# Residual stores on ScalarE's queue, and five smaller moves in a two-layer hybrid decoder step on one core

## The chip, the cores and the metric

The kernel runs on one core of one Trainium2 chip. The metric is device time in microseconds (us) of one execution, the median of several runs. Engines are named as in the profile: PE (matmul), PEld (PE's weight loads), DVE (vector), ACT (scalar, activations), POOL (GpSimd) and SP (here only an issuer of DMAs). A chip run of this kernel that differs by less than 0.3% (7.6 us) from another can't be told from it.

## The reference

One inference step of a two-layer decoder over 1032 tokens (1024 of a prompt, 8 samples of one token each), model width 1024, in float32:

```python
for l in range(DEPTH):                       # DEPTH = 2
    hn = _rmsnorm(x, norm_mix_g[l])
    if l < N_A:                              # layer 0: RG-LRU
        u = hn @ w_in_a[l]
        gate, xr, qm = u[..., :768], u[..., 768:1536], u[..., 1536:]
        xr, rc = _causal_dwconv(xr, rnn_conv0[l], ...)   # width 4
        y, hl = _rglru(xr, rnn_h0[l], ...)   # gates, a scan over tokens
        main = y * gelu(gate)
    else:                                    # layer 1: window-128 attention
        ...
    mem = _mem_attn(qm, mem_k[l], mem_v[l])  # 4 heads over 256 memory rows
    x = x + concat(main, mem) @ w_out[l]     # 1024 x 1024, the residual
    hn = _rmsnorm(x, norm_ffn_g[l])
    u = _causal_dwconv(hn @ w_ffn_up[l])     # 1024 x 6144, conv of width 3
    x = x + (gelu(u[..., :3072]) * u[..., 3072:]) @ w_ffn_down[l]
```

Beside the output of the trunk, the recurrent states (`yl`, the last conv inputs, and `rl`, the last scan values), the conv states and the keys and values are outputs of their own. The samples attend to memories of their own (`cache_mem_k`, `cache_mem_v`).

## The kernel before

**Arithmetic.** A float32 product runs as three matmuls in a reduced float32 type: an operand is split into a high part (a copy on ACT, `acopy`, L105) and a low part (the rest, a subtract on DVE, `vtt`, L113, or on POOL, `gtt`, L116). `mm3` then issues high by high (L298), high by low (L299) and low by high (L300). So each weight and each activation has to be loaded, copied by ACT and subtracted by DVE or POOL before PE can use it. A weight (`get`, `w_load` L251, `w_split`) is loaded up to two weights ahead by SP and split one ahead: its low part is always POOL's.

**Order.** One program, written as Python generators. `tick()` moves every open generator to its next `yield`, and one generator of a background list too. That order is the scheduler's input; for DVE, PE, POOL and SP (and ACT in the middle of layer 1) a scheduler then lines the instructions up, and on ACT in layer 0 and both FFNs they stay in the order of the program (`act_in_order(True)`). An engine runs its line in order, and so does SP with the DMAs that it issues: one that waits holds back all behind it. Big tiles (128 x 1032, "row") come from one pool of 44 buffers.

**Stages** (us of the profiled execution). Layer 0's RNN, 190 to 335: for six tiles of 128 channels the dense products of both branches, conv, gates and scan. Beside it the background list runs `sample_mem` (the samples' memory attention: scores, a transpose, a softmax on 32 rows, a second transpose on PE at L729, a masked copy on DVE, then products with the values, L749) and `ffn_prep`. Then `out_proj(0)`, 335 to 516; layer 0's FFN to 1250, its up-projection ending at about 1000; layer 1's mixer to 1624, `out_proj(1)` to 1779, and layer 1's FFN with its up-projection's end at about 2250.

**`out_proj`.** For each half of the tokens (`hb`), each of 8 output tiles `m` and each of two quarters `q` (258 columns): `get` the weight `m`, load the residual tile `x[m]` (in layer 0 by L772 from `x_t`, 516 KB; only in the first half), 24 matmuls, `vtt` of the sum into `x[m]` on DVE, then `on_tile`: a store of these 128 x 258 to `rD` in DRAM (L1323, 64 of them in both layers), a Square on ACT, and its sum on DVE. After a half, `norm(hf)` begins: it sums over partitions with a matmul by ones (L1335), takes the inverse root, scales, adds and splits the operands of the FFN (a chain of DVE, ACT and POOL), while the second half of `out_proj` runs on PE. `rD` is read back only at the FFN's end (`refill`).

**The last steps of the up-projection.** While its last tile's seven products run (`i` from 0 to 6), `fetch` loads the gated rows `gD[0]` to `gD[5]`, and `gated(j)` splits them for the down-projection: high on ACT, low on DVE (128 x 1032); the first down weight `dn.0.0` is loaded and split at step 4.

**Layer 1's mixer rows.** `load_m(b)` loads the mixer's output of token block `b` (0, 1, 2) from `mD` (L1820) and splits it. `mgetB` asks for a block when `out_proj(1)` first comes to its columns.

Of the kernel before, what the change touches and what calls it, by code (L numbers as in the profile page):

```python
# [18 lines left out]
NT = SEQ + NB  # L19
# [10 lines left out]
TIL = ((0, 1, 2), (3, 4, 5), (6, 7))  # L30
# [6 lines left out]
DCH = 6  # L37
# [12 lines left out]
def tile_trunk(ctx: ExitStack, tc: tile.TileContext, I: dict, O: list):  # L50
    nc = tc.nc
    mul, add, sub, amax = ALU.mult, ALU.add, ALU.subtract, ALU.max
# [31 lines left out]
    def ps():  # L84
        return pp.tile([P, 512], F32, tag="ps", name=nm("ps"))
# [26 lines left out]
    def vtt(out, a, b, op):  # L112
        return V.tensor_tensor(out=out, in0=a, in1=b, op=op)  # L113
# [12 lines left out]
    def f(ap):  # L126
        return ap.bitcast(F32)
# [22 lines left out]
    def spawn(g):  # L150
        t = Task(g)
        tasks.append(t)
        return t
# [116 lines left out]
    def get(key, ahead=1, load=1):  # L270
        i = widx[key]
        if Prep.fences and i >= Prep.fences[0]:
            Prep.fences.pop(0)
        end = (Prep.fences[0] if Prep.fences else len(W)) - 1
        top = min(end, i + ahead)
        while Prep.split <= top:
            while Prep.loaded <= min(end, Prep.split):
                w_load(Prep.loaded)
                Prep.loaded += 1
            w_split(Prep.split)  # L280
            Prep.split += 1
        while Prep.loaded <= min(end, top + load):
            w_load(Prep.loaded)
            Prep.loaded += 1
        return W[i]["t"]

    def load_w(n):
        while Prep.loaded < n:
            w_load(Prep.loaded)
            Prep.loaded += 1  # L290
# [399 lines left out]
    def sample_mem(l, dst):  # L690
        ck, cv = I["cache_mem_k"][l], I["cache_mem_v"][l]
        sc = sm()
        for hf in range(2):
            qb = row()
            SY.dma_start(qb[:, :1024], dbc(qmD[l][4 * hf : 4 * hf + 4, :], P, 1024))
            for pr in range(2):
                b0 = 4 * hf + 2 * pr
                kt = row()
                k4 = kt[:, :1024].rearrange("p (b k f) -> p b k f", b=2, k=2)
                for j in range(2):  # L700
                    SY.dma_start(k4[:, j], ck[b0 + j].rearrange("(k p) h d -> p k (h d)", p=P))
                yield
                for j in range(2):
                    q1 = qb[:, (2 * pr + j) * 256 : (2 * pr + j + 1) * 256]
                    gtt(k4[:, j], k4[:, j], q1[:, None, :].to_broadcast([P, 2, 256]), mul)
                yield
                for j in range(2):
                    V.tensor_reduce(
                        out=sc[:, :64].rearrange("p (k r) -> p k r", k=2)[:, :, (b0 + j) * 4 : (b0 + j) * 4 + 4],
                        in_=k4[:, j].rearrange("p k (h d) -> p k h d", h=4),  # L710
                        axis=AX.X,
                        op=add,
                    )
                yield
        yield
        yield
        t = ps()
        for k in range(2):
            T.transpose(t[:32, k * P : (k + 1) * P], sc[:, k * 32 : (k + 1) * 32], ident)
        yield  # L720
        n_, den, rd, pt = ty(), ty(), ty(), sm()
        V.tensor_reduce(out=n_[:32, :1], in_=t[:32, :256], axis=AX.X, op=amax, negate=True)
        act(pt[:32, :256], t[:32, :256], AF.Exp, bias=n_[:32, :1], accum_out=den[:32, :1])
        V.reciprocal(out=rd[:32, :1], in_=den[:32, :1])
        ts(V, pt[:32, :256], pt[:32, :256], rd[:32, :1], None, mul, None)
        yield
        t = ps()
        for k in range(2):
            T.transpose(t[:, k * 32 : (k + 1) * 32], pt[:32, k * P : (k + 1) * P], ident[:32, :32])  # L729
        bm32 = sm()  # L730
        SY.dma_start(bm32[:, :256], I["c_bm32"])
        pm = row()
        m4 = pm[:, :512].rearrange("p (k b r) -> p k b r", k=2, b=8)
        bm = bm32[:, :256].rearrange("p (b r) -> p b r", b=8)
        for k in range(2):
            vtt(m4[:, k], t[:, None, k * 32 : (k + 1) * 32].to_broadcast([P, 8, 32]), bm, mul)
        yield
        oc = sm()
        for pr in range(4):
            vt = row()  # L740
            v4 = vt[:, :1024].rearrange("p (b k f) -> p b k f", b=2, k=2)
            for j in range(2):
                SY.dma_start(v4[:, j], cv[2 * pr + j].rearrange("(k p) h d -> p k (h d)", p=P))
            yield
            yield
            o = ps()
            for j in range(2):
                for k in range(2):
                    T.matmul(  # L749
                        o[:32, :256], m4[:, k, 2 * pr + j], v4[:, j, k],  # L750
                        start=j == 0 and k == 0, stop=j == 1 and k == 1,
                    )
            for h in range(4):
                oh = o[:32, h * 64 : (h + 1) * 64]
                if pr == 0 and h == 0:
                    ts(V, oc[:32, :64], oh, hm32[:32, 0:1], None, mul, None)
                else:
                    stt(oc[:32, :64], oh, hm32[:32, h : h + 1], oc[:32, :64], mul, add)
            yield
        t = ps()  # L760
        T.transpose(t[:64, :32], oc[:32, :64], ident[:32, :32])
        t3 = t[:64, :32].rearrange("p (b h) -> p h b", h=4)
        for h in range(4):
            V.tensor_copy(out=dst(h), in_=t3[:, h])
        yield
# [9 lines left out]
    def out_proj(l, mget, ks, x, on_tile, on_half):  # L775
        for hb in range(2):
            for m in range(KD):
                key = f"out{l}.{hb}.{m}"
                wh, wl = get(key, 1, 1)
                if x[m] is None:  # L780
                    x[m] = residual(l, m)
                for q in (2 * hb, 2 * hb + 1):
                    c0 = QB[q]
                    p = ps()
                    mm3(p[:, :QW], [(wh[:, k * P : k * P + P], wl[:, k * P : k * P + P]) + mget(k, c0, QW) for k in ks])
                    vtt(x[m][:, c0 : c0 + QW], x[m][:, c0 : c0 + QW], p[:, :QW], add)
                    on_tile(q, m)
                    tick()
                drop(key)
            on_half(hb)  # L790
# [67 lines left out]
    def ffn(l, x, ops, need, weights, on_block, store=None):  # L858
# [84 lines left out]
        def gated(j):  # L943
            a = ga.pop(j)
            gh[j], gl[j] = row(F32R), row(F32R)
            acopy(gh[j][:, :NT], a[:, :NT])
            vtt(gl[j][:, :NT], a[:, :NT], f(gh[j][:, :NT]), sub)

        def refill(m):
            x[m] = row()  # L950
# [5 lines left out]
        for q, (j, name, hfs) in enumerate(SEQUENCE):  # L956
            if q == 6:
                load_pair(1)
            want = 7 if q < 10 else min(len(todo), q - 7 + AHEAD)
            while at < want:  # L960
                combine(*todo[at])
                at += 1
            t = product(j, name, hfs)
            if t is not None:
                last.append(t)
            tick()
            if j == KF - 1:
                i = STEADY.index(name)
                if i < DCH:
                    fetch(i)  # L970
                if i > 1:
                    gated(i - 2)
                if i == 4:
                    get(f"dn{l}.0.0", 0, 1)

        def down(c, m, b):
# [307 lines left out]
        tick()  # L1284
    bgfinish(smp)

    SY.dma_start(O[1], yl)
    SY.dma_start(O[2], rl)
    Mh, Ml = {}, {}
    ks_a = (6, 7, 0, 1, 2, 3, 4, 5)  # L1290

# [18 lines left out]
    def enter_ffn(l, x, mh, ml):  # L1310
# [8 lines left out]
        def cols(q):  # L1319
            return slice(QB[q], QB[q] + QW)  # L1320

        def on_tile(q, m):
            SY.dma_start(rD[l, m, :, cols(q)], x[m][:, cols(q)])  # L1323
            if m == 0:
                sums[q] = sm()
                act(sums[q][:, :QW], x[m][:, cols(q)], AF.Square)
            else:
                t = sm()
                act(t[:, :QW], x[m][:, cols(q)], AF.Square)
                vtt(sums[q][:, :QW], sums[q][:, :QW], t[:, :QW], add)  # L1330
# [95 lines left out]
    x = [None] * KD  # L1426
    ot, oh, need, ops, uw = enter_ffn(0, x, Mh, Ml)
    out_proj(0, mgetA, ks_a, x, ot, oh)
    Mh, Ml = {}, {}


# [401 lines left out]
    def start_m(b):  # L1833
        if b not in mload:
            while not {(i, e) for i in TIL[b] for e in range(2)} <= swa_done:
                tick()
            if b == 2:
                bgfinish(sst)
            mload[b] = spawn(load_m(b))
# [7 lines left out]

    x = [None] * KD
    start_m(0)
    get("out1.0.0", 1, 1)  # L1850
    for _ in range(6):
        tick()
# [139 lines left out]
```

## Time and profile before

| | before |
|---|---|
| median of 3 runs (lowest, highest) | 2533.32 us (2533.03, 2538.68) |
| the profiled execution: its time, its span | 2532.97 us, 2531.2 us |
| PE busy | 2336.5 us, 92% of the span |
| DVE, POOL, ACT busy | 61%, 56%, 44% |
| chain that ended last: PE, DVE, ACT | 34%, 7%, 2% |
| DMA moved | 273.64 MB, mean 108 GB/s |

The span is that of the trace; the 1.8 us between it and the time lie outside of the recorded work. PE's busy share is a mean over stages that differ: the views that follow cut the span into these stages.

### The profile page before, as it was taken

Reading aid. Unit: us, or ns where it says so; the run is one execution under the profiler, and the core shown is the slowest. Engines: PE = TensorE matmul, PEld = TensorE weight load, DVE = VectorE, ACT = ScalarE, POOL = GpSimd, SP = SyncE. Lnnn points to the kernel's source line nnn. Section 1 sums busy time; section 2 is a strip of 40 time slices with the busy share of each in tenths; the row PEclk is TensorE's granted clock in tenths of the full one; section 3 lists DMA queues with packets and bytes.
Section 4 is the critical chain, followed back from the end, with each engine's and each line's share of the span. In section 5 each row is a group of like instructions: output and inputs, shape, how many; then the busy total and the mean of one; then the engine's idle time right before and its main releaser. Section 6 shows DMA issues by size and latency. Waiting matters only on the chain. (4 is left out here: it accounts for less than half of the span.)

```text
span 2531.2 us, 42857 instructions
## 1 busy us (share of the span) xinstructions
PE 2336.5 (92%) x16590; PEld 2251.5 (89%) x16590; DVE 1549.6 (61%) x2826; ACT 1103.5 (44%) x2277; POOL 1428.0 (56%) x1123
## 2 busy tenths in 40 slices
PE   7997877799999999999989988787999999999999
PEld 5896866799999999999977787677999999999999
DVE  6658955666666666332478789875666566663321
ACT  5567753344433444211365577643443444442110
POOL 2149843588888885322144346435888888853220
PEclk9998989899999999999999999899999999999999
DMA  4221124212222225421575543551222222253311
GB/s 163 87 69 56 58 83 143 63 67 84 84 85 76 76 76 199 150 95 52 178 252 162 185 152 129 163 157 63 77 86 82 76 76 76 76 224 123 101 55 63
DMA packets 142491, 273.64 MB, mean 108 GB/s; under 512 B 28544, under 2 KB 85456, under 8 KB 142288
## 3 DMA queue, kind: packets, MB, share of 16 engines
q1 hardware_dynamic: 142288, 270.91, 31.9%
q8 instruction: 130, 2.13, 0.3%
q14 instruction: 73, 0.60, 0.1%
HBM read 211.99 MB, written 58.87 MB: 107 GB/s over the span
## 5 line engine op out<-in xcount | busy, mean ns | idle before, releaser
L116 POOL TENSOR_TENSOR row<-row,row 128x512 fp32r<-128x512 f32 (+9 forms) x754 | 1153.8, 1552 | 793.9 <-ACT row L105 476.4
L298 PE MATMUL ps<-row,row 128*128 128x258 f32 (+4 forms) x5032 | 1510.4, 303 | 55.5 <-ACT row L105 45.7
L299 PE MATMUL ps<-row,row 128*128 128x258 f32 (+4 forms) x5032 | 1509.1, 302 | 22.5 <-DVE row L113 18.7
L300 PE MATMUL ps<-row,row 128*128 128x258 f32 (+4 forms) x5032 | 1472.7, 301 | 23.5 <-POOL row L116 23.5
L298 PEld LDWEIGHTS ps<-row,row 128*128 128x128 f32 x5032 | 962.3, 191 | 73.9 <-ACT row L105 51.0
L299 PEld LDWEIGHTS ps<-row,row 128*128 128x128 f32 x5032 | 964.0, 192 | 40.2 <-DVE row L113 24.3
L300 PEld LDWEIGHTS ps<-row,row 128*128 128x128 f32 x5032 | 948.4, 192 | 34.1 <-POOL row L116 27.1
L105 ACT ACTIVATE row<-row 128x512 fp32r<-128x512 f32 (+8 forms) x768 | 505.4, 696 | 911.7 <-POOL row L116 305.4
L113 DVE TENSOR_TENSOR row<-row,ps 128x258 f32<-128x258 f32 (+2 forms) x736 | 322.3, 444 | 706.0 <-PE ps L300 666.5
L119 DVE SCALAR_TENSOR_TENSOR row<-row,fw,row 128x1023 f32<-128x1023 f32 x192 | 266.9, 1409 | 67.3 <-ACT row L105 67.3
L113 DVE TENSOR_TENSOR row<-row,row 128x258 fp32r<-128x258 f32 (+8 forms) x262 | 232.9, 912 | 31.3 <-ACT row L105 18.0
L105 ACT ACTIVATE row<-ps 128x258 f32<-128x258 f32 (+6 forms) x430 | 157.5, 406 | 69.6 <-PE ps L300 25.8
L116 POOL TENSOR_TENSOR row<-row,ty 128x768 f32<-128x768 f32 (+2 forms) x56 | 77.2, 1378 | 155.1 <-DVE ty L413 51.3
L105 ACT ACTIVATE row<-row,fw 128x1032 f32<-128x1032 f32 x96 | 114.9, 1245 | 68.8 <-DVE row L113 68.7
L105 ACT ACTIVATE sm<-row 128x258 f32<-128x258 f32 (+3 forms) x130 | 54.5, 452 | 153.5 <-DVE row L113 127.2
L113 DVE TENSOR_TENSOR row<-row,sb 128x8 f32<-128x8 f32 x96 | 102.3, 1066 | 0.0
L113 DVE TENSOR_TENSOR sm<-sm,sm 128x258 f32<-128x258 f32 (+5 forms) x125 | 81.9, 660 | 28.2 <-ACT sm L105 25.7
L105 ACT ACTIVATE row<-ps,ty,ty 128x256 f32<-128x256 f32 (+1 forms) x160 | 87.4, 564 | 10.1 <-DVE ty L113 7.6
L105 ACT ACTIVATE sm<-ps 128x384 f32<-128x384 f32 (+5 forms) x156 | 65.0, 444 | 39.2 <-PE ps L431 21.6
L113 DVE TENSOR_TENSOR row<-ps,row 128x384 fp32r<-128x384 f32 (+2 forms) x125 | 63.5, 519 | 25.1 <-ACT row L105 10.2
L119 DVE SCALAR_TENSOR_TENSOR row<-sm,pack,row 128x384 f32<-128x384 f32 (+1 forms) x54 | 62.6, 1162 | 14.6 <-POOL row L124 13.3
L116 POOL TENSOR_TENSOR sm<-sm,row 128x192 f32<-128x192 f32 (+3 forms) x72 | 49.5, 702 | 36.1 <-ACT sm L105 18.6
(163 smaller groups left out, 1497.3 us busy)
## 6 DMA issues: line engine op xcount, KB each, us to landing
row<-in_w_ffn_up SPq DMA_DIRECT2D x96, 512.0 KB, 3.3
gD<-row SPq DMA_DIRECT2D x48, 516.0 KB, 2.6
row<-gD SPq DMA_DIRECT2D x48, 516.0 KB, 5.6
row<-in_w_ffn_down SPq DMA_DIRECT2D x64, 384.0 KB, 3.1
row<-hD SPq DMA_DIRECT2D x48, 512.0 KB, 6.6
row<-in_w_out SPq DMA_DIRECT2D x32, 512.0 KB, 4.2
rD<-row SPq DMA_DIRECT2D x64, 129.0 KB, 1.9
row<-rD SPq DMA_DIRECT2D x16, 516.0 KB, 8.7
```

What stands on the lines that cost most here:

```text
L105: return nc.scalar.activation(out, in_, func, **kw)
L113: return V.tensor_tensor(out=out, in0=a, in1=b, op=op)
L116: return G.tensor_tensor(out=out, in0=a, in1=b, op=op)
L119: return V.scalar_tensor_tensor(out=out, in0=a, scalar=s, in1=b, op0=op0, op1=op1)
L298: T.matmul(out, ah, bh, start=first and j == 0, stop=False, skip_group_check=more)
L299: T.matmul(out, ah, bl, start=False, stop=False, skip_group_check=more)
L300: T.matmul(out, al, bh, start=False, stop=last and j == n - 1, skip_group_check=more)
```

## The change

Six edits, numbered here. (1) `sample_mem` (both layers) yields twice more between the softmax and the second transpose. (2) `gated(j)` does the low part of `j` = 0, 2, 4 on POOL, not on DVE. (3) `dn.0.0` and the weight after it are loaded from step 1 of the last tile, and `dn.0.0` is split at step 5. (4) The 64 stores to `rD` are issued by ACT, not by SP. (5) The stores of `yl` and `rl` stand behind `out_proj(0)` in the program. (6) In layer 1 a watcher generator starts `load_m(1)` and `load_m(2)` as soon as their rows are there.

```diff
@@ sample_mem
         ts(V, pt[:32, :256], pt[:32, :256], rd[:32, :1], None, mul, None)
+        yield
+        yield
         yield
         t = ps()
@@ ffn: gated, and the last tile of the up-projection
-            vtt(gl[j][:, :NT], a[:, :NT], f(gh[j][:, :NT]), sub)
+            (gtt if j < DCH and j % 2 == 0 else vtt)(gl[j][:, :NT], a[:, :NT], f(gh[j][:, :NT]), sub)
...
-                if i == 4:
+                if i == 1:
+                    load_w(widx[f"dn{l}.0.0"] + 2)
+                if i == 5:
                     get(f"dn{l}.0.0", 0, 1)
@@ ahead of out_proj(0)
-    SY.dma_start(O[1], yl)
-    SY.dma_start(O[2], rl)
     Mh, Ml = {}, {}
@@ enter_ffn: on_tile
-            SY.dma_start(rD[l, m, :, cols(q)], x[m][:, cols(q)])
+            nc.scalar.dma_start(rD[l, m, :, cols(q)], x[m][:, cols(q)])
@@ behind out_proj(0)
+    SY.dma_start(O[1], yl)
+    SY.dma_start(O[2], rl)
@@ layer 1, ahead of out_proj(1)
     start_m(0)
+
+    def ask_m():
+        for b in (1, 2):
+            while b not in mload:
+                if {(i, e) for i in TIL[b] for e in range(2)} <= swa_done and (b == 1 or sst.done):
+                    start_m(b)
+                else:
+                    yield
+
+    spawn(ask_m())
```

What the scheduler makes of it on the engines' lines (numbers in names are buffers, and differ between the kernels; lines of the kernel after the change are two to four higher).

SP's line at the start of `out_proj(0)`, before: `in_w_out` are its weights, `in_x_t` the residual tiles, `out<-yl` the state's store.

```order
L251 DMA row_3496<-in_w_out 128x1024
L1287 DMA out<-yl 128x54
L772 DMA row_3498<-in_x_t 128x1032
L1323 DMA rD<-row_3498 128x258 x2
L251 DMA row_3599<-in_w_out 128x1024
L772 DMA row_3601<-in_x_t 128x1032
L1323 DMA rD<-row_3601 128x258 x2
L251 DMA row_3667<-in_w_out 128x1024
L772 DMA row_3669<-in_x_t 128x1032
```

The same place of SP's line after the change.

```order
L251 DMA row_3491<-in_w_out 128x1024
L774 DMA row_3493<-in_x_t 128x1032
L804 DMA row_3528<-in_ffn_state 128x768
L1431 DMA out<-yl 128x54
L807 DMA out<-row_3528 1024x1x48
L251 DMA row_3597<-in_w_out 128x1024
L774 DMA row_3599<-in_x_t 128x1032
L251 DMA row_3665<-in_w_out 128x1024
L774 DMA row_3667<-in_x_t 128x1032
```

No store stands between the loads any more, and the first residual load stands ahead of the store of `yl`, which is still early. The stores now stand on ACT's line, each right ahead of the Square of its tile.

PE's line in the RNN stage, before: `ps_2693` takes the second transpose of `sample_mem`, `ps_2701` is a dense product, `ps_2674` and `ps_2680` are gates.

```order
L299 MATMUL ps_2674<-sm_2534,row_2374 128x384
L300 MATMUL ps_2674<-sm_2533,row_2374 128x384
L299 MATMUL ps_2680<-sm_2534,row_2374 128x384
L300 MATMUL ps_2680<-sm_2533,row_2374 128x384
L729 MATMUL ps_2693<-pack,sm_2623 128x32 x2
L298 MATMUL ps_2701<-row_126,row_2361 128x264
L299 MATMUL ps_2701<-row_134,row_2361 128x264
```

And where that transpose (now L731, `ps_2820`) stands after the change.

```order
L300 MATMUL ps_2761<-row_133,row_2546 128x384
L298 MATMUL ps_2801<-sm_2686,row_2558 128x384
L298 MATMUL ps_2807<-sm_2686,row_2558 128x384
L731 MATMUL ps_2820<-pack,sm_2623 128x32 x2
L298 MATMUL ps_2828<-row_126,row_2545 128x384
L299 MATMUL ps_2828<-row_134,row_2545 128x384
```

It moved back by 56 rows, behind the dense product of 264 columns, the gates of that block (`ps_2725`, `ps_2730`) and a dense product of 384 columns.

POOL's line at the end of layer 0's up-projection after the change: `row_10323` is the last up weight, `row_10457` and `row_10519` are low parts of down weights, the 128x1032 subtracts are `gated(0)`, `gated(2)` and `gated(4)`.

```order
L116 TENSOR_TENSOR row_10323<-row_10142,row_10323 128x512
L116 TENSOR_TENSOR row_10355<-row_10280,row_10354 128x1032
L116 TENSOR_TENSOR row_10421<-row_10352,row_10420 128x1032
L869 COPY ul<-row_10273 128x10
L116 TENSOR_TENSOR row_10457<-row_10318,row_10456 128x768
L869 COPY ul<-row_10311 128x10
L116 TENSOR_TENSOR row_10496<-row_10418,row_10495 128x1032
L116 TENSOR_TENSOR row_10519<-row_10320,row_10518 128x768
```

Before, none of the three 128x1032 subtracts stood there; all six were on DVE's line, which now has those of `gated(1)`, `gated(3)` and `gated(5)`.

## Rows read from the trace of the kernel before

**Rows 1.** Windows: from:to, length; busy of PE, PEld, DVE, ACT, POOL; PEclk; DMA.

```profile
600.00:650.00 50.00, 50.00 (x418) 50.00 (x417) 31.19 (x41) 22.07 (x36) 44.03 (x36) 1.00 0.18 64
190.00:335.00 145.00, 113.58 (x647) 105.17 (x647) 131.44 (x159) 113.58 (x161) 119.23 (x112) 0.91 0.18 55
335.00:412.00 77.00, 54.55 (x385) 51.59 (x386) 30.93 (x57) 23.35 (x49) 30.43 (x17) 0.85 0.42 130
412.00:516.00 104.00, 78.13 (x515) 72.95 (x515) 76.72 (x144) 40.49 (x98) 54.49 (x47) 0.83 0.24 76
976.00:1004.00 28.00, 23.65 (x159) 22.99 (x158) 20.65 (x28) 14.18 (x18) 11.92 (x7) 0.94 0.70 251
1624.00:1678.00 54.00, 49.71 (x384) 48.14 (x385) 38.24 (x74) 22.48 (x43) 22.66 (x13) 0.95 0.87 257
```

**Rows 2.** PE's waits, whole span: waited for, us in total, times, longest.

```profile
PE ps L300 <- POOL row L116: 23.5, 15, 5.0
PE ps L729 <- DVE sm L123: 12.6, 1, 12.6
```

**Rows 3.** SP's DMA issues, timeline from 335: start, length with its wait.

```profile
344.77 0.34 SPq L1287 DMA_DIRECT2D out<-yl  x1
345.21 0.38 SPq L772 DMA_DIRECT2D row<-in_x_t  x1
350.11 10.50 SPq L1323 DMA_DIRECT2D rD<-row  x2
360.70 0.38 SPq L251 DMA_DIRECT2D row<-in_w_out  x1
361.18 0.41 SPq L772 DMA_DIRECT2D row<-in_x_t  x1
366.67 0.80 SPq L1323 DMA_DIRECT2D rD<-row  x2
```

**Rows 4.** DVE and ACT, timeline from 349 to 368; in brackets the idle before.

```profile
349.65 0.42 DVE L113 TENSOR_TENSOR row<-row,ps 128x258 f32<-128x258 f32 x1 [3.64 <-DMA row<-in_x_t]
359.85 0.41 DVE L113 TENSOR_TENSOR row<-row,ps 128x258 f32<-128x258 f32 x1
366.21 0.76 DVE L113 TENSOR_TENSOR row<-row,ps 128x258 f32<-128x258 f32 x2 [5.96 <-DMA row<-in_x_t]
...
366.67 0.75 ACT L105 ACTIVATE sm<-row 128x258 f32<-128x258 f32 x2 [5.01 <-DVE row L113]
367.33 1.04 ACT L105 ACTIVATE row<-row 128x1024 fp32r<-128x1024 f32 x1
```

**Rows 5.** POOL and PE in the same half, timeline.

```profile
361.74 2.35 POOL L116 TENSOR_TENSOR row<-row,row 128x1024 fp32r<-128x1024 f32 x1 [2.11 <-ACT row L105]
...
364.14 0.39 PE L300 MATMUL ps<-row,row 128*128 128x258 f32 x1 [1.69 <-POOL row L116]
...
400.22 0.39 PE L300 MATMUL ps<-row,row 128*128 128x258 f32 x1 [1.12 <-POOL row L116]
411.56 1.66 PE L1335 MATMUL ps<-sm,ones 128*128 128x258 f32 x3 [5.79 <-DVE sm L113]
```

**Rows 6.** RNN stage, timelines of POOL and PE.

```profile
244.04 5.77 POOL L116 TENSOR_TENSOR sm<-row,sm 128x264 fp32r<-128x264 f32 x1 [0.88 <-ACT sm L105]
...
250.01 0.42 PE L729 MATMUL ps<-pack,sm 32*128 32x32 f32 x2 [12.59 <-DVE sm L123]
```

**Rows 7.** End of layer 0's up-projection, timelines of PE and DVE.

```profile
982.90 0.36 PE L298 MATMUL ps<-row,row 128*128 128x258 f32 x1 [2.00 <-DVE row L113]
...
978.66 3.77 DVE L113 TENSOR_TENSOR row<-row,row 128x1032 fp32r<-128x1032 f32 x2 [0.73 <-ACT row L105]
982.35 0.41 DVE L113 TENSOR_TENSOR row<-row,ps 128x258 f32<-128x258 f32 x1
982.68 1.22 DVE L113 TENSOR_TENSOR row<-row,row 128x1032 fp32r<-128x1032 f32 x1
```

**Rows 8.** Layer 1's `out_proj`, PE's timeline at the end of its first half.

```profile
1677.74 1.23 PE L1335 MATMUL ps<-sm,ones 128*128 128x258 f32 x2 [3.40 <-DVE sm L113]
```

## The prediction

> **What bounds the kernel now.** I read the windows by stage first, then PE's list of waits, then the timelines of the engines that release PE. In the middle of the FFN PE is busy for 50.00 of 50 us at the full granted clock, 1.00 (2.4 GHz) [rows 1]. The FFN's two long stretches can't be made faster by any of the six edits, since these change neither the number of matmuls nor their size. That leaves the places where PE stands idle: 31.4 us of the 145 us of the RNN stage, 22.5 of the 77 us of the first half of `out_proj(0)`, 25.9 of the 104 us of its second half, 4.3 of the 28 us at the up-projection's end in layer 0 (I count layer 1's like it), 4.3 of the 54 us of the first half of `out_proj(1)` [rows 1]. What one edit is worth is read from the wait that ends last in its own stage.
>
> The first half of `out_proj(0)` is the largest of them. A quarter tile is 24 matmuls; at full clock 418 take 50 us [rows 1], so 0.120 us each and 48 x 0.120 = 5.74 us for an output tile `m`. But the first matmul with the low weight (L300) of `m` = 2 starts at 364.14 and that of `m` = 7 at 400.22 [rows 5]: 36.08 / 5 = 7.22 us a tile. Both wait for POOL, as do those between them. That is not because POOL is busy: it has just waited for ACT, and takes 2.35 us [rows 5]. ACT's copy of the weight stands behind two Squares, the Squares wait for DVE's adds, and the adds wait 5.96 us for the residual tile's load [rows 4]. SP explains the load: it issues it at 361.18, because the pair of stores ahead of it held the queue from 350.11 for 10.50 us, until DVE's second add at 359.85 [rows 3, 4]. So it is a ring: store of `m` waits for the add of `m`, the load of `m`+1 waits behind the store, and the add of `m`+1 waits for the load, some 5 us after its issue.
>
> **Edits 4 and 5, in the first half of `out_proj(0)`.** SP's line now has the loads without stores between them. Three pieces:
> - The first residual load was issued at 345.21, right behind the store of `yl` at 344.77, and DVE waited for it until 349.65, idle for 3.64 us [rows 3, 4]. The load now stands ahead of that store. PE's tile must also be done; I take 3.0 of the 3.64. The splits of `Mh` and `Ml`, behind the Square on ACT, move up with it.
> - Five tiles at 7.22 us go to what sets them next. The chain from DVE's add is add 0.41, store's issue 0.40 (0.80 for two on SP [rows 3]; ACT's own price no row shows), Square 0.38 (0.75 for two), copy 1.04, POOL 2.35 [rows 4, 5]: 4.6 us, under PE's 5.74. So PE sets the pace: 5 x (7.22 - 5.74) = 7.4 us.
> - Before the sum over partitions PE waits 5.79 us (L1335 at 411.56 [rows 5]) because the last tile's load is late as well. Without that: add, issue, Square and DVE's sum, about 0.4 each, 1.6 us, and some 0.8 for semaphores: 2.4. Gain 3.4.
>
> Together 13.8 us. PE's own pace with the small waits inside a tile is probably nearer 6.2 than 5.74, which takes 2.3 back and more at the first tiles, where buffers are still scarce: I take **-11**. Bounds: -14 (all of it) and -3 (the first piece alone, if the loads then wait for buffers).
>
> The Trainium skill speaks against this term: in "DMA: Bandwidth & Descriptors", section "Issuing engines are not separate DMA queues", it says that DMAs started by several engines run on the same 16 DMA engines, and that spreading them saves only the sequencer's time to initiate them. By that alone the second and third piece would be nothing. The trace of before agrees about the transfers and shows what the sentence leaves out: the issuer holds up what stands behind a waiting DMA, 10.50 us at one pair.
>
> **The second halves, and ACT's new work.** The stores now stand on ACT's line, each ahead of the Square of the same tile. Both wait for the same add, so no new wait arises, only the issue: 16 in a half, 16 x 0.40 = 6.4 us. In the second half of `out_proj(0)` ACT is busy for 40.49 of 104 us [rows 1]; DVE, with 76.72, carries the chain of the norm. I take **0** here; bounds -2 and +6.4.
>
> **Edit 1, the second transpose.** PE stands for 12.59 us in front of it, until 250.01 [rows 2, 6]. It moves 56 rows back, behind a 264-column product and its gates. But the whole stall won't go: POOL makes the low part for that very block's gates from 244.04 to 249.81 [rows 6], so PE, in order, would next wait there, and DVE and POOL are busy for 131.44 and 119.23 of the stage's 145 us [rows 1]; DVE, nearly full, has its own work to finish before the stage ends. What PE gains is late next at DVE's scans. I take **-3**; bounds 0 and -12.6.
>
> **Edit 6, `out_proj(1)`.** Block 2's rows come earlier, inside the first half rather than at its end. PE is idle there for 4.3 of 54 us, with the DMA engines busy for 0.87 of the time, and waits 3.40 us at the end [rows 1, 8]. The stores on ACT free SP here too, but SP is not what PE waits for. I take **-2**; bounds -5 and +6.4 (16 issues on ACT).
>
> **Edits 2 and 3, the up-projection's ends.** PE waits 2.00 us at 982.90 for DVE, whose add at 982.35 came behind two low parts of 3.77 us in all [rows 7]; one alone takes 1.22 [rows 7], so one was stretched. Three of six low parts go to POOL, where the nearest row has 2.35 us (128 x 1024 [rows 5]). POOL is busy for 11.92 of these 28 us [rows 1], so it has the room. DVE loses 3 x 1.22 = 3.7 us, and the wait may shrink by 1 to 2. Against it: the low part of `dn.0.0` now stands behind two of them on POOL, 4.7 us later, and the low part of `gated(4)` comes 2.35 - 1.22 = 1.1 us later, just when PE comes to the first down-product. I take +0.5 a layer, **+1**; bounds -4 and +7.
>
> Here a rule weighs on the sum. The row shows two DVE subtracts of one form taking 3.77 us where 2 x 1.22 = 2.4 is expected [rows 7]. The Trainium skill, "SBUF — State Buffer", section "Who interferes with whom", calls DVE's second port pair shared with GpSimd, and an exclusive lock for whole instructions; the stretched row agrees. By that, each POOL low part holds DVE back.
>
> **Layer 1's mixer** is reordered by the scheduler around the two yields and the watcher. No row prices it: 0, and as bound a third of the largest single wait in PE's list, 12.6 / 3 = 4 us either way [rows 2].
>
> **Sum.** -11 + 0 - 3 - 2 + 1 + 0 = -15. The profiled execution took 2532.97 us, with a span of 2531.2, and lies 0.35 us under the median: 2533 - 15 = **2518 us**.
>
> **The rivals.**
> - *The transpose's stall goes whole.* For it: the gate behind it might find its operands, since POOL's 5.77 us there is itself a stretched row [rows 6], and a shifted DVE order might not stretch it. Against: DVE's busy share of 91%. 12.6 instead of 3: 2508 us.
> - *DVE is held by POOL at the two ends.* Three POOL subtracts block DVE for 3 x 2.35 = 7.1 us and take 3.7 of DVE's work away: +3.4 a layer, +6.8 instead of +1: 2524 us. For it: the stretched row [rows 7]. Against: POOL's first two run while PE still has products to do.
> - *The stores' move frees nothing but the first piece.* The loads then wait for buffers or for the adds, or the ring passes through ACT instead: -3 for -11, 2526 us, within 0.3% of before. For it: the chain of 4.6 us is close to 5.74, so an ACT issue of 1.5 us would close the ring again. Against: the adds wait for the load and for nothing else [rows 4]. The rule on issuing engines cited above would have it so.
> - *Slower: the issues lie on ACT's path in all halves.* ACT runs in order here and every weight split and norm split stands behind them. 64 x 0.40 = 25.6 us on the path, over the -15: 2543.6 us. It decides from 22.6 / 64 = 0.35 us a store on the path. For it: in the second halves ACT's copies release PE. Against: ACT is idle for 63.5 of 104 us there [rows 1], and in the first halves PE's 5.74 us cover the chain.
>
> **How the numbers follow.** My forecast has 0.54, the whole stall 0.10, the lock 0.10, no gain from the stores 0.17, slower 0.09. With 0.3% (7.6 us) as what a measurement can tell, faster means under 2525.7: 0.54 + 0.10 + 0.10 = 0.74; same 0.17; slower 0.09. The range, 2504 to 2532, holds the first four cases with the bounds of the reordering about them, 4 us below 2508 and 6 above 2526, and leaves out the slower case and the tails.
>
> **What would show it.** In the first half of `out_proj(0)`: L300 periods of 5.7 to 6.3 us without waits for POOL, DVE's adds released by PE and not by the load, L1335 about 11 us earlier, measured from the end of the RNN stage. ACT's stores at about 0.4 us each. At L731 a wait under 4 us, and the next wait at the gates of the same block. At the up-projection's ends PE idle within 1 us of before. The prediction is wrong if ACT's issue takes over 1 us, if the RNN stage ends later though the transpose no longer waits, or if layer 1's mixer differs by more than 4 us.

## The result, and the profile after

The changed kernel takes 2518.52 us (median of 4 runs, 2515.71 to 2519.54); the kernel before, run beside it, 2533.18 us. The ratio is 0.9935 with a 95% interval of 0.9918 to 0.9952, 12.2 to 20.8 us less; the medians are 14.7 us apart. Forecast were 2518 us and 2504 to 2532. The profiled execution has a span of 2517.7 us, 13.5 under that of before.

First the windows of the changed kernel, moved with its stages ([rows 1] are those of before; columns as there).

```profile
190.00:333.00 143.00, 114.37 (x638) 104.89 (x636) 128.30 (x157) 114.83 (x164) 116.79 (x106) 0.91 0.18 58
333.00:396.00 63.00, 54.18 (x387) 52.15 (x386) 34.78 (x60) 22.06 (x46) 27.90 (x16) 0.85 0.56 195
396.00:501.00 105.00, 77.12 (x511) 71.88 (x511) 76.49 (x145) 41.00 (x98) 54.25 (x46) 0.84 0.15 49
959.50:987.50 28.00, 25.33 (x180) 24.25 (x179) 22.57 (x26) 13.52 (x16) 17.32 (x10) 1.00 0.72 252
```

PE does the same 54 us of work in the first half of `out_proj(0)`, in 63 instead of 77 us. The second half is no shorter. At the up-projection's end PE is busy for 25.33 of 28 us, against 23.65.

How the difference is spread can be worked out from the starts of the same matmuls in both traces. The table has stage lengths; the last columns are of experiments that follow (differences from the profiled execution of before, us).

| stage, ended by | before | changed | stores alone | loads ahead, SP | changed, stores on SP | changed, layer 1 without yields |
|---|---|---|---|---|---|---|
| to the first matmul of `out_proj(0)` | 335.28 | -2.27 | -0.41 | -0.82 | -2.24 | -1.86 |
| first half, to the first L1335 | 76.28 | -13.78 | -10.33 | -10.00 | -4.27 | -15.28 |
| second half, to the first up-product | 75.19 | +1.58 | +0.85 | -0.04 | +0.38 | +1.48 |
| up-projection, to 75 us ahead of its end | 427.52 | +0.37 | +0.77 | +1.10 | -0.30 | +0.09 |
| its end, to the 61st down-product | 121.32 | -2.55 | -1.25 | -1.00 | -2.39 | -2.55 |
| rest of the FFN and layer 1's mixer | 579.29 | +6.90 | +2.94 | +2.79 | +10.52 | +2.78 |
| `out_proj(1)`, both halves | 133.44 | -1.55 | -3.19 | -0.33 | -3.66 | -1.73 |
| layer 1's up-projection, without its end | 428.43 | +0.01 | -0.32 | -0.23 | -0.40 | +0.16 |
| its end | 107.63 | -2.07 | -0.05 | -1.36 | -2.68 | -2.59 |

The first half of `out_proj(0)` in the changed kernel: SP's loads, ACT with its stores, DVE's adds, PE (start, length, in brackets the idle before and what ended it).

```profile
323.91 0.38 SPq L774 DMA_DIRECT2D row<-in_x_t  x1
...
341.57 0.34 SPq L1431 DMA_DIRECT2D out<-yl  x1
343.43 0.46 SPq L774 DMA_DIRECT2D row<-in_x_t  x1
350.29 0.33 SPq L774 DMA_DIRECT2D row<-in_x_t  x1
351.20 0.37 SPq L774 DMA_DIRECT2D row<-in_x_t  x1
...
366.35 0.33 ACTq L1325 DMA_DIRECT2D rD<-row  x1
...
343.52 0.42 DVE L113 TENSOR_TENSOR row<-row,ps 128x258 f32<-128x258 f32 x1 [1.18 <-PE ps L300]
363.25 0.42 DVE L113 TENSOR_TENSOR row<-row,ps 128x258 f32<-128x258 f32 x1 [1.70 <-PE ps L300]
368.99 0.42 DVE L113 TENSOR_TENSOR row<-row,ps 128x258 f32<-128x258 f32 x1 [1.39 <-PE ps L300]
374.75 0.43 DVE L113 TENSOR_TENSOR row<-row,ps 128x258 f32<-128x258 f32 x1 [1.41 <-PE ps L300]
...
358.80 0.58 PE L300 MATMUL ps<-row,row 128*128 128x258 f32 x1 [1.69 <-POOL row L116]
389.20 0.28 PE L300 MATMUL ps<-row,row 128*128 128x258 f32 x1
395.51 0.70 PE L1337 MATMUL ps<-sm,ones 128*128 128x258 f32 x2 [0.85 <-DVE sm L113]
```

No add waits for a load any more (where a wait is shown, it is for PE); before, an add waited 5.96 us for its load [rows 4]. The adds of the first quarters of `m` = 2, 3 and 4 (363.25, 368.99 and 374.75) stand 5.74 and 5.76 us apart: PE's own pace. In `m` = 2 PE still waits 1.69 us for POOL. The first residual load is issued at 323.91, ahead of the store of `yl`, and the others well ahead of their use; a store costs ACT 0.33 us, and the wait ahead of the partition sum (now L1337) is 0.85 instead of 5.79 us [rows 5].

PE's waits in the RNN stage, at the up-projection's end and in layer 1's mixer of the changed kernel.

```profile
241.88 0.81 PE L298 MATMUL ps<-sm,row 128*128 128x264 f32 x2 [4.49 <-ACT sm L105]
264.95 0.81 PE L298 MATMUL ps<-sm,row 128*128 128x264 f32 x2 [3.75 <-ACT sm L105]
332.85 0.23 PE L763 MATMUL ps<-pack,sm 32*64 32x32 f32 x1 [6.71 <-DVE row L113]
...
967.76 0.36 PE L298 MATMUL ps<-row,row 128*128 128x258 f32 x1 [0.93 <-DVE row L113]
983.64 0.44 PE L298 MATMUL ps<-row,row 128*128 128x384 f32 x1 [1.42 <-ACT row L105]
...
1398.75 1.02 PE L751 MATMUL ps<-row,row 128*32 128x256 f32 x4 [3.62 <-DMA row<-in_cache_mem_v]
```

The 12.59 us in front of the transpose [rows 6] are gone; 4.49 us of it came back at once at the gates behind it, and 3.75 at another block's. The 6.71 us at the stage's end are not new: before, PE waited there as long, one matmul later. At the up-projection's end PE waited three times before: 2.00 us [rows 7], and twice at the first down-products. The rows of before:

```profile
335.28 0.58 PE L298 MATMUL ps<-row,row 128*128 128x258 f32 x1 [6.60 <-ACT row L105]
...
997.34 0.45 PE L299 MATMUL ps<-row,row 128*128 128x384 f32 x1 [0.78 <-DVE row L113]
1002.48 0.44 PE L300 MATMUL ps<-row,row 128*128 128x384 f32 x1 [1.58 <-POOL row L116]
```

The 2.00 us became 0.93; the 0.78 and 1.58 are gone, and a wait of 1.42 us for ACT and a short one (0.19, shown further below) are new. The last row of the changed kernel is new too: PE waits for the samples' values, which it didn't before.

### The profile page after: what moved, and what is told of

Its sections match the earlier page's. It is cut to its first block, busy times and chain, and to the rows that moved or that the text cites. A ratio compares the mean times of both kernels' runs of the same rounds, so it can differ in the third digit from the quotient of the medians.

```text
span 2517.7 us, 42880 instructions
## 1 busy us (share of the span) xinstructions
PE 2337.0 (93%) x16590; PEld 2253.7 (90%) x16590; DVE 1558.1 (62%) x2820; ACT 1104.2 (44%) x2277; POOL 1440.6 (57%) x1129
## 5 line engine op out<-in xcount | busy, mean ns | idle before, releaser
L116 POOL TENSOR_TENSOR row<-row,row 128x512 fp32r<-128x512 f32 (+9 forms) x760 | 1166.9, 1558 | 777.5 <-ACT row L105 464.7
L300 PE MATMUL ps<-row,row 128*128 128x258 f32 (+4 forms) x5032 | 1470.6, 301 | 16.8 <-POOL row L116 16.8
L300 PEld LDWEIGHTS ps<-row,row 128*128 128x128 f32 x5032 | 946.6, 192 | 27.6 <-POOL row L116 20.1
```

What stands on the lines that cost most here:

```text
L116: return G.tensor_tensor(out=out, in0=a, in1=b, op=op)
L300: T.matmul(out, al, bh, start=False, stop=last and j == n - 1, skip_group_check=more)
```

## The experiments

Each kernel was run beside the kernel before; ratios are to that one, with their 95% interval in brackets. The intervals come from several runs of each kernel, so they can separate differences below the 0.3% of a single run. Stage lengths are from one profiled execution of each kernel.

**Edit 4 alone.**

```diff
-            SY.dma_start(rD[l, m, :, cols(q)], x[m][:, cols(q)])
+            nc.scalar.dma_start(rD[l, m, :, cols(q)], x[m][:, cols(q)])
```

> The kernel before with edit 4 alone: the 64 stores to rD are issued by ACT. Theory (the stores' wait held the residual and weight loads on SP's queue): the period of an output tile in the first half of out_proj(0) falls from 7.22 to about 5.75 us and the wait of 5.79 us ahead of the partition sum goes, so about 11 us less in that half; the first residual load still stands behind the store of yl, so the first add still waits for its load. In all 2533 - 11 = about 2522 us; the up-projection's ends and layer 1's mixer as before. Rival (the stores' move frees nothing, since all DMAs share the same engines, and the gain came from the other edits): 2530 to 2533 us.

2522.55 us, 0.9951 (0.9935 to 0.9966). The first half is 10.3 us shorter, as the theory says; the rival falls. The changed kernel has 3.5 us beyond it in this half; here the first residual load still stands behind the store of `yl` (later runs bear on that).

**Edit 4 taken back.**

> The changed kernel with edit 4 taken back: the stores are issued by SP again, all other edits stay. Theory: the first half of out_proj(0) is back at 7.2 us a tile and has its wait of some 5 us ahead of the partition sum; the RNN stage (-2) and the up-projection's ends (-4.5) keep their gains and layer 1's mixer its loss (+7), so about 2531 us. Rival (the other edits make the gain together with the earlier first load): 2520 us.

2527.36 us, 0.9972 (0.9960 to 0.9985), the theory's side, though its figure is 3.6 us too high. Without edit 4 DVE's adds wait for their loads again, 7.2 us apart:

```profile
367.57 0.76 DVE L113 TENSOR_TENSOR row<-row,ps 128x258 f32<-128x258 f32 x2 [5.79 <-DMA row<-in_x_t]
374.73 0.76 DVE L113 TENSOR_TENSOR row<-row,ps 128x258 f32<-128x258 f32 x2 [5.48 <-DMA row<-in_x_t]
```

The half is still 4.3 us shorter than before: its first load is early here.

**The order of SP's line without another issuer.**

```diff
-                wh, wl = get(key, 1, 1)
-                if x[m] is None:
-                    x[m] = residual(l, m)
+                wh, wl = get(key, 1, 1 if l or hb else 3)
+                for k in range(m, m + 1 if l or hb else min(m + 3, KD)):
+                    if x[k] is None:
+                        x[k] = residual(l, k)
```

> The kernel before, stores on SP as before; in the first half of out_proj(0) alone the residual tiles and weights are asked for two tiles earlier, so that two more loads stand ahead of each pair of stores in SP's line. It tells the order of the queue from the issuer. Theory (a load behind a store that waits): adds no longer wait for their load although SP issues everything, the tile's period falls to 5.75 to 6 us and the half is 8 to 11 us shorter: about 2523 us. Rival (ACT as second issuer is what helps, or PE's pace is set by ACT's and POOL's weight splits): period stays above 7 us, 2531 to 2534 us.

2523.07 us, 0.9957 (0.9943 to 0.9972): the same as with edit 4 alone, and the half 10.0 us shorter against 10.3, with SP issuing every DMA. SP's line waits at its stores as before, and DVE no longer notices:

```profile
369.99 2.93 SPq L1324 DMA_DIRECT2D rD<-row  x2
373.01 0.38 SPq L251 DMA_DIRECT2D row<-in_w_out  x1
373.48 0.41 SPq L772 DMA_DIRECT2D row<-in_x_t  x1
...
369.54 0.42 DVE L113 TENSOR_TENSOR row<-row,ps 128x258 f32<-128x258 f32 x1 [1.48 <-PE ps L300]
372.14 0.42 DVE L113 TENSOR_TENSOR row<-row,ps 128x258 f32<-128x258 f32 x1 [0.83 <-PE ps L300]
375.01 0.42 DVE L113 TENSOR_TENSOR row<-row,ps 128x258 f32<-128x258 f32 x1 [1.53 <-PE ps L300]
```

So what counted was that a load stood behind a store that waits, not who issues.

**Twice the issues on ACT.**

```diff
-            nc.scalar.dma_start(rD[l, m, :, cols(q)], x[m][:, cols(q)])
+            for h in (0, 129):
+                cs = slice(QB[q] + h, QB[q] + h + 129)
+                nc.scalar.dma_start(rD[l, m, :, cs], x[m][:, cs])
```

> The changed kernel with each store to rD split into two of 129 columns: 128 instead of 64 issues on ACT, the same bytes. An issue takes 0.33 us of ACT in the changed kernel, 64 x 0.33 = 21 us more of ACT. Theory (the issues are covered: PE's 5.74 us a tile in the first halves, ACT's idle time in the second): within 4 us of the changed kernel, 2518 to 2522 us; any loss lies in the second halves. Rival (the issues lie on ACT's path everywhere): 2518 + 21 = 2539 us.

2525.00 us, 0.9964 (0.9951 to 0.9977), some 6 us over the changed kernel: between the two, nearer to the theory, whose 4 us it misses. A pair takes 0.81 us and more. By the medians less than a third of the 21 us is on the path. In the traces it is less: the two halves of `out_proj(0)` are 2.3 and 1.4 us longer than in the changed kernel, those of `out_proj(1)` 1.9 longer and 2.3 shorter, 3.3 us together.

```profile
368.48 0.81 ACTq L1327 DMA_DIRECT2D rD<-row  x2
374.22 1.07 ACTq L1327 DMA_DIRECT2D rD<-row  x2
```

**Edit 2 alone, edit 3 alone, and both** (each on the kernel before; the lines are those of the change).

> The kernel before with edit 2 alone: the low parts of gated(0), gated(2) and gated(4) on POOL. It tells which of edits 2 and 3 shortens the up-projection's ends, which took 2.5 us less in layer 0 and 2.0 us less in layer 1 with all edits. Theory (DVE is freed of three subtracts, so its adds out of PSUM come sooner, although POOL's instructions stretch its own): both ends 1 to 2.5 us shorter, 2533 - 3.5 = about 2530 us. Rival (POOL's subtracts hold DVE's back, and the gain is edit 3's): ends 0 to 3 us longer, 2533 to 2537 us.

2535.01 us, 1.0014 (1.0004 to 1.0025): slower by 3.5 us, the rival's side. In its profiled execution the ends are not longer (1.3 and 0.3 us shorter, though PE's idle time in layer 1's grew by 1.1 us), and the 3.5 us can't be placed there; the mixer, whose code is that of before, is 4.6 us longer.

> The kernel before with edit 3 alone: the first two down weights are loaded from step 1 of the last tile and the first is split at step 5. Theory (edit 2 makes the gain): the waits for POOL and DVE of about 1 to 2 us at the ends stay, or only the last one, 1.58 us for POOL's low part of a down weight, goes: 2530 to 2533 us. Rival (the ends waited for the weights' load): 2 us less at each end, 2529 us.

2533.61 us, 1.0001 (0.9991 to 1.0010): nothing.

> The kernel before with edits 2 and 3 together. Alone, edit 2 moved PE's wait from the last up-products to the first down-products (POOL's low part of the first down weight now stands behind two gated low parts), and edit 3 alone changed nothing. Theory (the two need each other: with the down weights loaded and split in the new order, POOL's two early subtracts fall into the time in which PE still has up-products): each end 2 to 2.5 us shorter and nothing lost at the first down-products, 2533 - 4.5 = about 2528.5 us. Rival (the ends' gain in the changed kernel comes from the shift of all the rest): 2532 to 2535 us.

2529.45 us, 0.9978 (0.9968 to 0.9988): 5.6 us less. In the traces the two need each other: PE's idle time at the two ends changes by -0.2 and +1.1 us with edit 2 alone, by -0.1 and -0.1 with edit 3 alone, and by -1.2 and -1.1 with both. That accounts for 2.3 of the 5.6 us; the rest is not placed. PE's waits at layer 0's end with edit 2 alone, then with both:

```profile
981.71 0.36 PE L298 MATMUL ps<-row,row 128*128 128x258 f32 x1 [1.08 <-DVE row L113]
995.49 0.45 PE L299 MATMUL ps<-row,row 128*128 128x384 f32 x1 [1.60 <-POOL row L116]
998.60 0.45 PE L298 MATMUL ps<-row,row 128*128 128x384 f32 x1 [1.43 <-ACT row L105]
```

```profile
983.27 0.36 PE L298 MATMUL ps<-row,row 128*128 128x258 f32 x1 [1.42 <-DVE row L113]
990.46 0.45 PE L300 MATMUL ps<-row,row 128*128 128x384 f32 x1 [0.21 <-POOL row L116]
999.18 0.44 PE L298 MATMUL ps<-row,row 128*128 128x384 f32 x1 [1.42 <-ACT row L105]
```

With edit 2 alone the wait for DVE halves, but PE then waits 1.60 us for POOL's low part of `gated(4)`, which it does not with both.

**The extra yields by layer.** First the changed kernel with them in layer 0 alone.

```diff
-        yield
-        yield
+        if not l:
+            yield
+            yield
         yield
         t = ps()
```

> The changed kernel with the two extra yields of sample_mem in layer 0 alone. Theory: in layer 1 the yields shift the values' products of sample_mem in PE's order, to a place where PE waits for their load (3.62 us at L751) and for what follows; without them the mixer loses 1 to 3 us against the kernel before, as with the stores alone, rather than 6.9: 2514 us. Rival (the mixer's loss comes from another edit, or from the shift of the start alone): within 2 us of the changed kernel, 2517 to 2520 us.

2511.02 us, 0.9915 (0.9901 to 0.9929): 7.5 us under the changed kernel by the medians, some 5 us by the ratios, whose intervals overlap a little; it is the fastest of all. Then the same two lines alone, on the kernel before: in layer 0, and in layer 1 (`if l`).

> The kernel before with two extra yields in sample_mem in layer 0 alone. Theory: they are what shortened the RNN stage by 2.3 us: PE's 12.6 us wait at the second transpose goes and is spread over waits for ACT's and DVE's part of the gates, since DVE is busy for nine tenths of the stage; 2531 us. Rival (the transpose's wait goes whole): 2521 us; other rival (nothing left, since DVE sets the stage's end): 2533 us.

2529.80 us, 0.9984 (0.9974 to 0.9995). The RNN stage is 2.5 us shorter, as expected. In the profiled execution, which at 2525.04 us lies below the median, the first half of `out_proj(0)` is 5.1 us shorter too, with the stores still on SP: the scheduler, with the yields, puts the first residual load ahead of the store of `yl`, although the program has them in the old order:

```profile
324.36 0.38 SPq L775 DMA_DIRECT2D row<-in_x_t  x1
341.39 0.34 SPq L1290 DMA_DIRECT2D out<-yl  x1
```

> The kernel before with the two extra yields of sample_mem in layer 1 alone. Theory: they alone cost layer 1's mixer 4 to 5 us, at the stretch in which PE comes to the values' products and to the query products behind them; 2533 + 4.5 = about 2537.5 us. Rival (the loss in the changed kernel was one of place, and needs the shift of the earlier edits): 2531 to 2534 us.

2543.20 us, 1.0037 (1.0024 to 1.0050): 9.4 us slower, twice what the theory says. The wait at the values' products is there, on an otherwise unchanged kernel:

```profile
1411.71 1.02 PE L752 MATMUL ps<-row,row 128*32 128x256 f32 x4 [2.63 <-DMA row<-in_cache_mem_v]
```

The mixer's stage is 6.1 us longer, `out_proj(1)` 6.9.

**The changed kernel without the watcher.**

```diff
-    spawn(ask_m())
```

> The changed kernel without edit 6, the watcher; PE's order is the same. In layer 1's out_proj the last tile of the first half and the wait ahead of the second took 12.1 us before, 9.8 us with the stores on ACT alone, 8.4 us with all edits. Theory (the stores give two thirds of it, the watcher the rest): that stretch 9.5 to 10 us, 1 to 1.5 us slower than the changed kernel, 2519.5 us. Rival (the watcher does it all, and the earlier loads of block 2 are what counts): 12 us, 2522 us; other rival (the watcher does nothing): 2518 us.

2517.42 us, 0.9935 (0.9921 to 0.9949): the last tile of the first half of `out_proj(1)` and the partition sum behind it take 8.1 us without the watcher, against 8.4 with it and 12.1 before. It gives nothing that can be measured. The stores on SP with the watcher (9.2 us there) are not slow either, so edit 4 isn't shown to be the cause.

**One extra yield in layer 0, none in layer 1.**

```diff
-        yield
-        yield
+        if not l:
+            yield
         yield
         t = ps()
```

> The changed kernel with one extra yield in layer 0's sample_mem and none in layer 1's: the transpose stands 26 rows of PE's line earlier than with two. Theory (DVE, busy for nine tenths of the RNN stage, sets its end): the RNN stage ends within 2 us of that with two yields, and 2510 to 2513 us in all. Rival (the transpose still waits for the softmax there): 2 to 6 us slower, 2513 to 2517 us.

2517.73 us, 0.9939 (0.9925 to 0.9954), 6.7 us over two yields, though the RNN stage is 3.0 us shorter than before in this execution, more than with two. The rival's time, but not its place: with one yield the scheduler puts the store of `yl` ahead of the first residual load again, and the first half waits.

```profile
340.57 0.36 SPq L1431 DMA_DIRECT2D out<-yl  x1
341.02 0.38 SPq L251 DMA_DIRECT2D row<-in_w_out  x1
341.49 0.38 SPq L774 DMA_DIRECT2D row<-in_x_t  x1
...
347.39 0.42 DVE L113 TENSOR_TENSOR row<-row,ps 128x258 f32<-128x258 f32 x1 [5.58 <-DMA row<-in_x_t]
```

## Why the prediction was right, and where it was not

The total is right to half a microsecond, and that is luck in part. The largest term holds in its mechanism, and four sizes are off: in the profiled executions the first half of `out_proj(0)` and the up-projection's ends gave 8.4 us more than forecast, layer 1's mixer and the second half of `out_proj(0)` 8.5 us less. Two of the signs that the prediction named went against it: the mixer differs by more than 4 us, and PE's idle time at the ends is 1.7 and 1.2 us less than before, not within 1 us of it.

**First half of `out_proj(0)`, -11: measured -13.8.** The three pieces before the discount were 3.0 + 7.4 + 3.4 = 13.8. That this sum was met is chance. Between the same matmuls the first piece (to the first L300 of `m` = 2) measures 25.8 instead of 28.9 us, the second (on to that of `m` = 7) 30.4 instead of 36.1, the third (on to the sum) 6.3 instead of 11.3: gains of 3.1, 5.7 and 5.0. In the second piece the tiles from `m` = 3 on need no discount, they run at 5.75 us; but `m` = 2 waits 1.69 us for POOL, and behind that wait PE's matmuls start 0.215 us apart for a stretch (the lower level of the clock, 1.2 GHz) instead of 0.12, which costs 1.5 us. The changed kernel without yields in layer 1 and the one without the watcher have the wait without that stretch, and gain 15.3 and 15.4 us in the half. In the third piece the wait was put at 2.4 us, with 0.8 for semaphores that no row shows; it is 0.85, and 0.24 at the second sum.

Edit 4 alone gives 10.3, and the same order on SP alone gives 10.0. The Trainium skill ("DMA: Bandwidth & Descriptors", "Issuing engines are not separate DMA queues") says that DMAs of several issuers run on the same 16 DMA engines and that a second issuer saves only the sequencer's time to initiate them. The first part fits: a store lands 1.9 us after its issue (median) from SP and from ACT. The trace of before could say nothing on it, since SP issues every DMA there. What the prediction drew from the second part, that the second and third piece would be nothing, fell: the gain lies in what stands behind a waiting store. One attribution failed: the first piece was put down to edits 4 and 5, but it is the yields of edit 1 that bring the first load ahead of the store of `yl` (both runs with two yields and stores on SP have it, the run with edit 5 and one yield has not).

**Second halves and ACT's issues, 0: +1.6 in layer 0**, and +0.9 with edit 4 alone. Inside the bounds. An issue costs 0.33 us, not 0.40; how much of it is on the path the doubling gives only roughly (3 to 6 of 21 us).

**The transpose, -3: measured -2.3** (-2.5 with the yields alone). One execution misleads by about 1 us here: six profiled executions with both yields in layer 0 average -1.7 in this stage against before, seven without any in layer 0 average -0.5, so some 1.2 us are the yields'. The rival that the stall goes whole fell: PE waits next at the gates of the block, as argued, for ACT's high part rather than POOL's low.

**`out_proj(1)`, -2: measured -1.6.** The sign holds, its reason doesn't: the watcher gives nothing. What shortens the end of the first half by 2 to 4 us in several kernels stays open; among six kernels with the stores on SP and neither the watcher nor yields in layer 1 it varies by 2 us (10.7 to 12.7).

**The ends, +1: measured -2.6 and -2.1.** This term has the wrong sign. The step that failed is the cost of "the low part of `dn.0.0` now stands behind two of them on POOL, 4.7 us later", and with it that of `gated(4)`. POOL does make it later: before, it was ready 2.0 us ahead of PE's first down-product (988.24 against 990.25), now it is 1.2 us behind that product's start (974.86 against 973.62). But the product begins with the weight's high part, and its first matmul with the low part waits only 0.19 us; for `gated(4)` PE doesn't wait at all.

```profile
962.52 9.41 POOL L116 TENSOR_TENSOR row<-row,row 128x512 fp32r<-128x512 f32 x4 [2.98 <-ACT row L105]
973.03 1.83 POOL L116 TENSOR_TENSOR row<-row,row 128x768 fp32r<-128x768 f32 x1
974.92 0.44 PE L300 MATMUL ps<-row,row 128*128 128x384 f32 x1 [0.19 <-POOL row L116]
```

The first row ends with `gated(0)` and `gated(2)`, the second is the down weight. The prediction also left out the two waits behind the first, 0.78 and 1.58 us, which went. Not all of -4.6 is the edits', though. Of the 2.6 and 2.1 us the fall in PE's idle time is 1.7 and 1.2. Five profiled executions without these two edits, that of before among them, average -0.6 at layer 0's end against before, seven with both -2.4: the same 1.7 us of the 2.6. The rest is the clock (below). That POOL holds DVE back is seen in the changed kernel: an add of 128 x 8 on DVE beside POOL's subtract takes 2.40 us, otherwise 0.17.

```profile
976.83 0.17 DVE L113 TENSOR_TENSOR row<-row,sb 128x8 f32<-128x8 f32 x1
978.11 2.40 DVE L113 TENSOR_TENSOR row<-row,sb 128x8 f32<-128x8 f32 x1
977.78 2.70 POOL L116 TENSOR_TENSOR row<-row,row 128x1032 fp32r<-128x1032 f32 x1 [2.77 <-ACT row L105]
```

That agrees with "SBUF — State Buffer", "Who interferes with whom", of the Trainium skill, by which a DVE instruction with two inputs in SBUF contends with a GpSimd instruction that reads SBUF; PE just doesn't wait for it there.

**Layer 1's mixer, 0 with 4 either way: measured +6.9.** The step that failed is "No row prices it: 0". Edit 1 acts in both layers and only layer 0's transpose was priced. The yields in layer 1 are the cause: five kernels with them have +6.1 to +10.5 here, nine profiled executions without them 0 to +4.6 (means 7.4 and 2.3, the latter counting before's own 0), and taking them out of the changed kernel gives 4.1 us here. They shift the values' products to a place at which their load, issued among others, comes 2.4 to 3.6 us late; in the nine others PE doesn't wait for it. The wait is not the whole loss. The stretch in before and in the changed kernel:

```profile
1035.59:1614.88 579.29, 534.61 (x3314) 492.78 (x3313) 371.36 (x980) 274.51 (x791) 218.34 (x202) 0.97 0.45 146
1018.94:1605.13 586.19, 538.72 (x3315) 498.98 (x3313) 373.35 (x980) 274.62 (x790) 218.34 (x202) 0.96 0.44 145
```

Only 2.8 of the 6.9 us are more idle time of PE; in the other 4.1 the same matmuls take longer, at a granted clock of 0.96 instead of 0.97. With the yields of layer 1 alone it is the other way round: 7.8 us more idle time, matmuls 1.7 us shorter. What the reordering does behind the wait isn't taken apart here; nor is the further loss in `out_proj(1)` with the yields alone.

## What to carry to other kernels

A queue that issues in order makes a load wait for a store's data: look at what stands behind each waiting DMA, and move either the load ahead or the store to another line; both gave 10 us here. Price an edit of a shared helper once for each place that calls it: the same two lines gave 1 to 2.5 us in one layer's stage and took at least 4 in the other's. And where a scheduler lines up the work, test each edit alone and with its neighbours: of two edits one gave nothing alone and the other cost 3.5 us, and together they gave 5.6, of which the traces show 2.3 as less idle time of PE.

## What was not expected of the hardware

The same wait of PE can cost the clock or not. In the profiled execution of before PE waits 2.00 us at 982.90 [rows 7] and the window around it has a granted clock of 0.94 [rows 1]; behind the wait its matmuls of 258 columns start 0.215 us apart for a stretch instead of 0.12, the lower level of 1.2 GHz. With edit 3 alone the wait is 1.98 us, and the clock stays at 1.00 in the windows around both ends:

```profile
976.00:1004.00 28.00, 23.72 (x170) 23.06 (x170) 22.04 (x29) 14.74 (x18) 12.36 (x7) 1.00 0.74 262
2238.00:2267.00 29.00, 24.67 (x177) 24.01 (x177) 22.71 (x29) 15.22 (x18) 13.95 (x7) 1.00 0.76 279
```

Each such end is about 1.5 us shorter than before's (-1.45 and -1.57) although PE's idle time in it is the same to 0.1 us, so a stage compared in one execution of each kernel is uncertain by that much.
